# Token sums among the query products, first keys in a spare bank; layer-1 low halves and a fourth head's scaling on GpSimd

## The chip, the cores and the metric

The kernel runs on one core of a Trainium2 chip. The metric is the device time of one execution in microseconds (us). The engines that matter are TensorE (PE: matrix products, with PEld for the loads of its weights), VectorE (DVE), ScalarE (ACT), GpSimd (POOL) and the DMA queues, most of which SyncE (SP) issues. TensorE writes its results into eight PSUM banks.

## The reference, cut to what matters

Two layers of a decoder trunk on 512 tokens of width 1024, all in fp32. Only the parts that the change touches are shown.

```python
def rms_norm(x, g):
    y = x * rsqrt(mean(x * x, axis=-1, keepdims=True) + EPS)
    return y * g

# layer 0: q, k, v (8 heads of 64) and three convolution parts come from one projection
proj = rms_norm(x, g) @ w_in                       # 1024 -> 3*512 + 3*512
a_out = stick_breaking_attention(heads(q), heads(k), heads(v))
b_out = short_conv_mixer(b_gate, c_gate, u, conv_w)
x = x + concatenate([a_out, b_out]) @ w_out
x = x + swiglu(rms_norm(x, g2))                     # hidden width 2816

# layer 1: 16 query heads, 4 key/value heads of 64, an indexer that selects keys
q, k = rms_norm(q, q_gain), rms_norm(k, k_gain)     # per head of 64
score = sum_h w_idx[h] * relu(q_idx[h] @ k_idx.T)   # causal; the top 128 keys of each query count
logits = q @ k.T * HEAD_DIM ** -0.5 + rel_bias      # others -inf
p = softmax(logits)
x = x + (p @ v) @ w_out
x = x + swiglu(rms_norm(x, g3))
```

## The kernel before

**Products in halves.** Every fp32 matrix is split into a high half (rounded to fp32r) and a low half (what the rounding left), and each product is made of three TensorE products: high by high, high by low, low by high (`mm3`, L104). So for each operand there is one operation that makes the high half, a cast on ScalarE, and one that makes the low half, a subtraction, mostly on VectorE. Weights arrive by DMA in a tile `raw` (three buffers, pool `wraw`); `halves` (L159) makes `wh` on ScalarE (L163) and `wl` on VectorE (L164), three buffers each. `plan` and `split_next` split the weights of the next projection ahead of time.

**Banks.** Projections take PSUM banks in turn from a list, `self.banks` ('dbca' from here on); `few_banks(...)` sets another list. Beside a, b, c and d there are o and t, which attention uses, and two buffers z.

**Order.** In the start of layer 0 and in the mixer of layer 1 the order on TensorE, VectorE, ScalarE and GpSimd is the written one (`manual_schedule(engines=L1_ORDER)`); elsewhere a scheduler orders. Written order is made with slots: `self.after(n, fn, key)` runs fn n slots later, among others that are due by the key. Names such as LAG_TQ are such numbers.

**Start of layer 0.** `queries` (L411) transposes the tokens chunk by chunk (`turn_x`, L399), splits each chunk and accumulates four query products in the banks d, b, c and a, over five spans of chunks, whose weights `halves(i)` splits. Then `first_rstd` (L451) sums the squares of each token on VectorE (L458, four sums of a 128x1024 block), and makes the reciprocal root `rcol` and four diagonal blocks from it (L462 to L469). `stack` (L481) then moves the query products into the arena: high halves by ScalarE (L487), low halves by VectorE (L491), two of each to a bank. The first keys (`k_proj(0)`), the values V (`proj_tm(W, 1024, ...)`, evacuated by ScalarE L188 and VectorE L189) and the other keys follow. `first_rbc`, `setup_rest` and `bias_table` are small products and copies of the setup between them.

**Mixer of layer 1.** The blocks of keys/values and of two halves of the queries (`hf` 0 and 1) come out of `proj_tm` and are copied by ScalarE (`ev_kv` L996, `ev_q0`). `squares` (L933) makes the sums of squares of each head: below the limit `SQ_ACT` with one ScalarE square and accumulator for each head, above it with one square of the block and a VectorE reduction (L954, L955). `norm` scales each block by the heads' roots on GpSimd (L975). Then `turn_k` (L1012) and `turn_q` (L1028) transpose by TensorE into bank t or o (`pt`, L987) and make both halves of the result:

```python
if K_POOL:                      # turn_k; before: K_POOL is False
    src = sp.tile([P, S], F32, name="qt", tag="tmp", bufs=1)
    nc.scalar.activation(src, pt, AF.Copy, scale=gk)
    nc.scalar.copy(kh[:, g], src)
    nc.gpsimd.tensor_tensor(kl[:, g], src, khf[:, g], op=ALU.subtract)
    return
nc.scalar.activation(kh[:, g], pt, AF.Copy, scale=gk)                 # L1020
self.after(LAG_KLO, lambda: nc.vector.scalar_tensor_tensor(           # L1021
    kl[:, g], pt, gk, khf[:, g], op0=ALU.mult, op1=ALU.subtract), -1)
```

In `turn_q` a column c in `Q_POOL[hf]` goes the same way, by a ScalarE copy `qt` and a GpSimd low half (L491 in `stack`); the others read `pt` on VectorE. VectorE searches the top keys at that time (L922, L925; the masks L928).

The attention of layer 1 runs over 16 steps n, four query blocks for each of four key heads; a step has four heads r. `logits` (L1055) loads the bias of a head when its first block comes (L1066, on SP's queue, four buffers), makes z and adds bias and maximum on VectorE (L1073); `exps` is on ScalarE; `norms` (L1086) scales each head by its reciprocal sum (L1090), on GpSimd for r in `NORM_POOL` (L1093), on ScalarE for r in `NORM_ACT` (L1096), else on VectorE (L1098). `turn_p` (L1101) transposes the four heads on TensorE (L1106), and `prod` multiplies by V.

Of the kernel before, what the change touches and what calls it, by code (L numbers as in the profile page):

```python
# [8 lines left out]
F32 = mybir.dt.float32  # L9
F32R = mybir.dt.float32r  # L10
ALU = mybir.AluOpType
# [4 lines left out]
P = 128  # L16
S = 512
D = 1024
KC = D // P
TB = S // P  # L20
# [9 lines left out]
LAG_Z = 14  # L30
PRE, PRE_CUT, PRE_STORE = 20, 8, 5
LAG_K, T1P, B2, LAG_KLO, P1 = 2, 3, 'adbc', 2, 0
EARLY, SQ_ACT = 3, 0
DOT_PACE = 1
DBL_ACT, K_POOL = True, False
PACE = (4.8, 5.0, 5.3)
NORM_POOL, NORM_ACT = (1,), (3,)
Q_POOL = ((1,), (2, 3))
# [7 lines left out]
EARLY = 2  # L46
T1P = 4
LAG_K = 3
NORM_POOL = (0, 1)
NORM_ACT = (3,)  # L50
LAG_CH = 4
LAG_TQ = 5
Q_POOL = ((2,), (2, 3))
B2 = 'dbca'
LAG_N = 8
LAG_TK = 8
# [3 lines left out]
LAG_W = 4  # L60
LAG_C = 11
LAG_DOT = 5
K_POOL = False

def rel_buckets():

# [11 lines left out]
class Net:  # L78
# [329 lines left out]
        self.split(self.xh3(c), ps, g=self.g_mix(0, c))  # L408
        return lambda: nc.scalar.copy(self.xT[:, c], ps)

    def queries(self, W, raws):  # L411


        xs = self.xs
        self.qps = ps = [self.acc() for _ in range(4)]
        ws = []

        def halves(i):
            a, b = X_SPANS[i]
            raw = raws[i] if i < 3 else self.load_raw(W[a * P:b * P, 0:512].rearrange(  # L420
                "(k p) n -> p k n", p=P), b - a, 512)
            ws.append(self.halves(raw, b - a, 512))

        def dot(i, ms):
            a, b = X_SPANS[i]
            for m in ms:
                c = slice(m * P, (m + 1) * P)
                for k in range(a, b):
                    h, l = xs[k]
                    self.mm3(ps[m], ws[i][0][:, k - a, c], ws[i][1][:, k - a, c], h, l, k == 0,  # L430
                             k == KC - 1)

        keep = self.turn_x(0)
        halves(0)
        keep1 = self.turn_x(1)
        keep()
        halves(1)
        keep1()
        for i in range(5):
            dot(i, (0, 1))  # L440
            n = 2 + 2 * i
            if n < KC:
                keep = self.turn_x(n)
            dot(i, (2, 3))
            if n < KC:
                keep1 = self.turn_x(n + 1)
                keep()
                halves(i + 2)
                keep1()

    def first_rstd(self, xp):  # L451

        nc = self.nc
        xt = self.x_tm
        ss = xp.tile([P, TB], F32, name="ss")
        junk = xp.tile([P, D], F32, name="junk")
        for tb in range(TB):
            nc.vector.tensor_tensor_reduce(out=junk, in0=xt[:, tb], in1=xt[:, tb], scale=1.0,  # L458
                                           scalar=0.0, op0=ALU.mult, op1=ALU.add,
                                           accum_out=ss[:, tb:tb + 1])  # L460
        t = xp.tile([P, TB], F32, name="t4")
        nc.vector.tensor_scalar(ss, ss, 1.0 / D, EPS, op0=ALU.mult, op1=ALU.add)  # L462
        nc.scalar.activation(self.rcol, ss, AF.Abs_reciprocal_sqrt)
        self.newton(self.rcol, ss, t)
        nc.vector.tensor_scalar(self.rq[:, 0:TB], self.rcol, -0.125, None, op0=ALU.mult)
        nc.vector.tensor_scalar(self.rq[:, TB:], self.rcol, 0.125, None, op0=ALU.mult)
        dg = self.cst.tile([P, S], F32, name="sqx", tag="sqx")
        for tb in range(TB):
            nc.vector.tensor_scalar(dg[:, tb * P:(tb + 1) * P], self.ident,  # L469
                                    self.rcol[:, tb:tb + 1], None, op0=ALU.mult)  # L470
        return dg
# [128 lines left out]
    def layer0_mix(self):  # L600
# [8 lines left out]
        with self.tc.tile_pool(name="xin", bufs=1) as xp:  # L609

            raws = self.load_x(xp, W)
            with self.tc.manual_schedule(engines=L1_ORDER):
                self.queries(W, raws)
                self.plan(self.fm_tiles(W, 512, P, KC, P, 8, 1, None))
                dg = self.first_rstd(xp)
                for m in range(4):
                    qs = self.R(32 + 4 * m, 2, S)
                    self.stack([(qs[0][:, e], qs[1][:, e]) for e in range(2)], self.qps[m])
                    heads.append(qs[0])
# [8 lines left out]
        with self.tc.tile_pool(name="l0", bufs=1) as sp:  # L628
# [5 lines left out]
            def k_proj(i):  # L634
                b = 64 + 8 * (i % 3)
                (kd, kdf), kl = self.R(b, 2, S), self.R(b + 4, 2, S)[0]

                def ev_k(m, ps):
                    kt = sp.tile([P, S], F32, name="kt", tag="ct0")
                    nc.vector.tensor_tensor(kt, ps, self.rbc, op=ALU.mult)  # L640
                    for e in range(2):
                        own, oth = slice(64 * e, 64 * e + 64), slice(64 - 64 * e, 128 - 64 * e)
                        nc.scalar.copy(kd[own, e], kt[own])
                        nc.gpsimd.tensor_copy(kd[oth, e], kt[own])
                        nc.vector.tensor_tensor(kl[own, e], kt[own], kdf[own, e], op=ALU.subtract)
                self.proj_fm(W, 512 + i * P, P, xs, ev_k, gcols=P, per=8)
                return kd, kl
# [38 lines left out]

            st = self.stream(self.stick(heads, keys, sp, state), RATE0)
            for i in range(4):
                keys.append(k_proj(i))
                self.after(LAG0, more_keys)  # L690
                if i == 0:
                    self.proj_tm(W, 1024, xs, ev_v)
                    self.after(LAG0, lambda: state.update(v=True))
                    self.few_banks("ad")
                    state["acc"] = True
# [132 lines left out]
    def layer1_mix(self):  # L828
# [15 lines left out]
        with ExitStack() as es:  # L844
# [167 lines left out]
            def turn_k(g):  # L1012
                pt = turn(kn, g, "to"[g % 2])
                if K_POOL:
                    src = sp.tile([P, S], F32, name="qt", tag="tmp", bufs=1)
                    nc.scalar.activation(src, pt, AF.Copy, scale=gk)
                    nc.scalar.copy(kh[:, g], src)
                    nc.gpsimd.tensor_tensor(kl[:, g], src, khf[:, g], op=ALU.subtract)
# [4 lines that stand above are left out]
# [5 lines left out]
            def turn_q(qn, hf, c, tag):  # L1028
                pt = turn(qn, c, tag)

                if c in Q_POOL[hf]:
                    src, eng = sp.tile([P, S], F32, name="qt", tag="tmp", bufs=1), nc.gpsimd
                    nc.scalar.copy(src, pt)
                else:
                    src, eng = pt, nc.vector
                self.stack([(qs[:, h], qsf[:, h]) for h in (8 * hf + 2 * c, 8 * hf + 2 * c + 1)],
                            src, eng, LAG_LO)
# [190 lines left out]
```

## Time and profile before

| | |
|---|---|
| median of 3 runs | 1220.45 us (1219.55 to 1222.16) |
| profiled execution | 1221.7 us, its span 1219.8 us |
| TensorE busy | 1191.4 us, 98% |
| TensorE weight loads | 981.4 us, 80% |
| VectorE busy | 661.2 us, 54% |
| ScalarE busy | 477.8 us, 39% |
| GpSimd busy | 118.1 us, 10% |
| mean granted TensorE clock | 0.994 |

The times of the runs are those of whole executions. The profile is of one execution, and its span runs from the first to the last instruction. Busy time is summed over the span, so it tells how full an engine is on the whole and not which engine holds up the others at a place; that is read from the timeline and from the waits. The granted clock is given as a share of the full one; 0.50 is the lower of the two levels.

### The profile page before, as it was taken

The page shows a single profiled execution, that of the slowest core. Times are in us where ns is not written, and L with a number is a line of the kernel's source. Part 1 is how long each engine was busy: PE and PEld are TensorE (multiplying, and loading weights), DVE is VectorE, ACT ScalarE, POOL GpSimd, SP SyncE. Part 2 cuts the span into 40 slices and gives each one's busy share as a digit, 9 for nine tenths or more (in the row PEclk, how much of TensorE's full clock was granted, in tenths as well). Part 3 has the DMA queues.
Part 4 walks back from the last instruction along what each step waited for, and adds up shares of the span by engine and source line. Part 5 has one row for each costly group of instructions (what it writes and reads, how often), then busy time and mean ns, then how long its engine had stood idle before and what let it go on. Part 6 is the DMA issues. An engine that isn't in the chain of part 4 may idle for free.

```text
span 1219.8 us, 14608 instructions
## 1 busy us (share of the span) xinstructions
PE 1191.4 (98%) x5547; PEld 981.4 (80%) x5547; DVE 661.2 (54%) x1081; ACT 477.8 (39%) x778; POOL 118.1 (10%) x191
## 2 busy tenths in 40 slices
PE   9899999999999999999999889999999999999998
PEld 7677778888888888888788678888888888888886
DVE  4679975665555534333379978755434344342322
ACT  5457643554343422222252279644322232322120
POOL 1135310200000000011001134112000000000000
PEclk9899999999999999999999999999999999999999
DMA  6231225878788632233536431213333333333330
GB/s 188 76 87 52 70 70 174 269 257 288 266 264 284 227 104 78 95 98 95 172 139 229 150 104 36 70 69 121 87 104 87 97 94 89 101 97 93 125 100 35
DMA packets 118582, 159.85 MB, mean 131 GB/s; under 512 B 6292, under 2 KB 91840, under 8 KB 118512
## 3 DMA queue, kind: packets, MB, share of 16 engines
q1 hardware_dynamic: 117712, 157.73, 40.4%
q10 hardware_dynamic: 800, 1.18, 0.3%
q8 instruction: 44, 0.72, 0.3%
q14 instruction: 26, 0.21, 0.1%
HBM read 131.00 MB, written 27.89 MB: 130 GB/s over the span
## 4 chain that ended last, share of the span: by engine, by line
PE 87%; DVE 8%; issue 2%; ACT 2%; POOL 1%; POOLq 0%; DVEq 0%; ACTq 0%
PE acc L106 22%; PE acc L108 21%; PE acc L107 21%; PE acc L234 5%; PE acc L235 5%; PE acc L233 5%; DVE w L922 1%; PE z L500 1%; PE pt L1106 1%; PE z L501 1%; DVE L L925 1%; PE po L107 1%; DVE om L525 1%; PE po L108 1%; PE po L106 1%
## 5 line engine op out<-in xcount | busy, mean ns | idle before, releaser
L106 PE MATMUL acc<-arena,wh 128*128 128x512 f32 (+2 forms) x1176 | 466.5, 397 | 7.5 <-DVE arena L491 5.6
L108 PE MATMUL acc<-arena,wl 128*128 128x512 f32 (+2 forms) x1176 | 460.7, 392 | 0.1
L107 PE MATMUL acc<-arena,wh 128*128 128x512 f32 (+2 forms) x1176 | 458.9, 390 | 0.0
L164 DVE TENSOR_TENSOR wl<-raw,wh 128x1024 fp32r<-128x1024 f32 (+1 forms) x167 | 202.7, 1214 | 288.0 <-ACT wh L163 287.7
L163 ACT CAST wh<-raw 128x1024 fp32r<-128x1024 f32 (+1 forms) x167 | 173.1, 1037 | 360.4 <-PE acc L107 153.7
L106 PEld LDWEIGHTS acc<-arena,wh 128*128 128x128 f32 (+1 forms) x1176 | 221.5, 188 | 52.7 <-ACT arena L487 6.0
L108 PEld LDWEIGHTS acc<-arena,wl 128*128 128x128 f32 (+1 forms) x1176 | 221.1, 188 | 48.3 <-DVE wl L164 0.4
L107 PEld LDWEIGHTS acc<-arena,wh 128*128 128x128 f32 (+1 forms) x1176 | 221.3, 188 | 45.2 <-issue 0.7
L233 PE MATMUL acc<-wh,arena 128*128 128x512 f32 x272 | 108.9, 400 | 0.0
L234 PE MATMUL acc<-wl,arena 128*128 128x512 f32 x272 | 108.2, 398 | 0.0
L235 PE MATMUL acc<-wh,arena 128*128 128x512 f32 x272 | 108.0, 398 | 0.0
L235 PEld LDWEIGHTS acc<-wh,arena 128*128 128x128 f32 x272 | 51.6, 190 | 12.1
L803 DVE TENSOR_TENSOR pwl<-praw,pwh 128x1024 fp32r<-128x1024 f32 (+1 forms) x25 | 30.2, 1206 | 56.7 <-ACT pwh L802 56.7
L234 PEld LDWEIGHTS acc<-wl,arena 128*128 128x128 f32 x272 | 51.6, 190 | 11.5
L233 PEld LDWEIGHTS acc<-wh,arena 128*128 128x128 f32 x272 | 51.5, 189 | 11.4
L751 DVE TENSOR_TENSOR ft<-acc,rbc 128x512 f32<-128x512 f32 x44 | 30.1, 690 | 46.2 <-PE acc L108 46.1
L287 POOL TENSOR_TENSOR ssq<-ssq,sqx 128x512 f32<-128x512 f32 x12 | 18.2, 1516 | 371.7 <-ACT sqx L286 371.7
L802 ACT CAST pwh<-praw 128x1024 fp32r<-128x1024 f32 (+1 forms) x25 | 25.9, 1035 | 69.0 <-DMA praw<-in_od_w_in_dram 37.4
L753 ACT ACTIVATE fs<-ft 128x512 f32<-128x512 f32 x44 | 27.6, 629 | 51.3 <-DVE ft L751 51.2
L500 PE MATMUL z<-arena 128*128 128x384 f32 (+3 forms) x120 | 41.1, 345 | 4.6 <-DVE mx L1073 3.8
L758 DVE TENSOR_TENSOR fp<-acc,fs 128x512 f32<-128x512 f32 x44 | 30.4, 691 | 24.0 <-PE acc L108 24.0
L1073 DVE CUSTOM_DVE_ANT_0 L<-z,bias 128x128 f32<-128x128 f32 (+3 forms) x64 | 30.6, 485 | 18.2 <-PE z L1072 17.4
(210 smaller groups left out, 1263.6 us busy)
## 6 DMA issues: line engine op xcount, KB each, us to landing
raw<-in_ffn_w_gate_dram SPq DMA_DIRECT2D x44, 512.0 KB, 3.8
raw<-in_ffn_w_up_dram SPq DMA_DIRECT2D x44, 512.0 KB, 3.8
raw<-in_ffn_w_down_dram SPq DMA_DIRECT2D x42, 512.0 KB, 3.6
l1h<-pwh SPq DMA_DIRECT2D x24, 512.0 KB, 2.7
l1l<-pwl SPq DMA_DIRECT2D x24, 512.0 KB, 3.0
wh<-l1h SPq DMA_DIRECT2D x24, 512.0 KB, 4.4
wl<-l1l SPq DMA_DIRECT2D x24, 512.0 KB, 4.3
raw<-in_ev_w_in_dram SPq DMA_DIRECT2D x23, 512.0 KB, 3.8
```

The costliest lines, as they stand in the source:

```text
L106: mm(ps, wh, xh, start=first, stop=False)
L107: mm(ps, wh, xl, start=False, stop=False)
L108: mm(ps, wl, xh, start=False, stop=last)
L163: nc.scalar.copy(wh, raw)
L164: (lo or nc.vector).tensor_tensor(wl, raw, wh.bitcast(F32), op=ALU.subtract)
L233: mm(ps[tb], h[:, t], wh[:, k], start=c == 0, stop=False)
L234: mm(ps[tb], h[:, t], wl[:, k], start=False, stop=False)
L235: mm(ps[tb], l[:, t], wh[:, k], start=False, stop=c == kc - 1)
L500: self.nc.tensor.matmul(z, qs, kd, start=True, stop=False)
L758: nc.vector.tensor_tensor(p, ps, sil[m], op=ALU.mult)
L803: nc.vector.tensor_tensor(l, raw, h.bitcast(F32), op=ALU.subtract)
L1073: nc.vector.tensor_tensor_reduce(out=u["ls"][:, r], in0=z, in1=bias[h][:, 0:nk][:, ::-1], scale=1.0, scalar=FILL, op0=ALU.add, op1=ALU.max ...
```

## The change

1. The four sums of squares become a function `sums`, called in `queries` after the second and the third span, two sums each. `first_rstd` uses what they leave.
2. The first keys (i = 0) are accumulated in bank o instead of the next bank in turn, and V starts at the first bank of the list.
3. The first weight of V is split ahead together with the weight of the first keys.
4. `SQ_ACT` goes from 0 to 256: the squares of the key heads are made with ScalarE's accumulator, head by head.
5. `K_POOL` is switched on: the low halves of the keys are made by GpSimd from a ScalarE copy. All four columns of the first query half go the same way (`Q_POOL`). The copies `qt` lie in the buffers of the raw weights instead of a buffer of their own.
6. The scaling of the fourth head (r = 3) goes from ScalarE to GpSimd.

```diff
-EARLY, SQ_ACT = 3, 0
+EARLY, SQ_ACT = 3, 256
-DBL_ACT, K_POOL = True, False
+DBL_ACT, K_POOL = True, True
-NORM_POOL = (0, 1)
-NORM_ACT = (3,)
+NORM_POOL = (0, 1, 3)
+NORM_ACT = ()
-Q_POOL = ((2,), (2, 3))
+Q_POOL = ((0, 1, 2, 3), (2, 3))
-K_POOL = False
...
                 keep()
                 halves(i + 2)
                 keep1()
+            if 0 < i < 3:
+                self.sums(xp, (2 * i - 2, 2 * i - 1))
+
+    def sums(self, xp, tbs):
+
+        nc = self.nc
+        if self.ss is None:
+            self.ss = xp.tile([P, TB], F32, name="ss")
+            self.junk = xp.tile([P, D], F32, name="junk")
+        for tb in tbs:
+            nc.vector.tensor_tensor_reduce(out=self.junk, in0=self.x_tm[:, tb],
+                                           in1=self.x_tm[:, tb], scale=1.0, scalar=0.0,
+                                           op0=ALU.mult, op1=ALU.add,
+                                           accum_out=self.ss[:, tb:tb + 1])
...
-                self.plan(self.fm_tiles(W, 512, P, KC, P, 8, 1, None))
+                self.plan(self.fm_tiles(W, 512, P, KC, P, 8, 1, None)
+                          + self.tm_tiles(W, 1024, KC, None)[0:1])
...
             for i in range(4):
+                if i == 0:
+                    self.few_banks("o")
                 keys.append(k_proj(i))
+                if i == 0:
+                    self.few_banks(None)
...
-                    src = sp.tile([P, S], F32, name="qt", tag="tmp", bufs=1)
+                    src = self.wraw.tile([P, S], F32, name="qt", tag="raw")
...
-                    src, eng = sp.tile([P, S], F32, name="qt", tag="tmp", bufs=1), nc.gpsimd
+                    src, eng = self.wraw.tile([P, S], F32, name="qt", tag="raw"), nc.gpsimd
```

How the instructions stand on the engines is shown at three places. The first is VectorE at the end of the query products, before: `wl` is a weight's low half, L189 the low half of a token chunk, L458 a token sum, L462 the first step of the root.

```order
L189 SCALAR_TENSOR_TENSOR arena<-pstat,cols,arena 128x512 x2
L164 TENSOR_TENSOR wl<-raw,wh 128x1024 x2
L458 ISA junk,ss<-x_tm 128x1024
L458 ISA ss 128x1
L458 ISA junk,ss<-x_tm 128x1024
L458 ISA ss 128x1
L164 TENSOR_TENSOR wl<-raw,wh 128x1024
L458 ISA junk,ss<-x_tm 128x1024
L458 ISA ss 128x1
L458 ISA junk,ss<-x_tm 128x1024
L458 ISA ss 128x1
L462 TENSOR_SCALAR ss<-ss 128x4
```

The same place after the change, where line numbers differ a little (L460 is the sum, L163 the weight, L469 the first step of the root).

```order
L460 ISA junk,ss<-x_tm 128x1024
L460 ISA ss 128x1
L460 ISA junk,ss<-x_tm 128x1024
L460 ISA ss 128x1
L188 SCALAR_TENSOR_TENSOR arena<-pstat,cols,arena 128x512 x2
L163 TENSOR_TENSOR wl<-raw,wh 128x1024
L460 ISA junk,ss<-x_tm 128x1024
L460 ISA ss 128x1
L460 ISA junk,ss<-x_tm 128x1024
L460 ISA ss 128x1
L163 TENSOR_TENSOR wl<-raw,wh 128x1024 x2
L469 TENSOR_SCALAR ss<-ss 128x4
```

Two sums now stand ahead of the last two token chunks and two behind the last query weight; the weights of the keys and of V follow both and stand ahead of the root.

The second place is TensorE between the last query product (acc_124) and the first key product (acc_387), before, with the engines that an instruction waits for.

```order
L106 MATMUL acc_124<-arena_81,wh_256 128x512
L107 MATMUL acc_124<-arena_81,wh_256 128x512
L108 MATMUL acc_124<-arena_81,wl_257 128x512
L106 MATMUL acc_387<-arena_81,wh_311 128x512 [waits DVE_49,PE_49,Activation_49]
L107 MATMUL acc_387<-arena_81,wh_311 128x512
L108 MATMUL acc_387<-arena_81,wl_312 128x512
```

The same place after the change, where the keys' product is acc_393.

```order
L105 MATMUL acc_124<-arena_81,wh_260 128x512
L106 MATMUL acc_124<-arena_81,wh_260 128x512
L107 MATMUL acc_124<-arena_81,wl_261 128x512
L105 MATMUL acc_393<-arena_81,wh_317 128x512 [waits Activation_49]
L106 MATMUL acc_393<-arena_81,wh_317 128x512
L107 MATMUL acc_393<-arena_81,wl_318 128x512 [waits DVE_49]
```

The products stand in the same order; the first key product waits for ScalarE's half of its weight alone, and the third for VectorE's half.

The third place is GpSimd in the first six steps of the layer-1 attention, after the change: L987 scales a query block by its roots, L1105 scales a head of the attention by its reciprocal sum (L1093 before), L498 is a query's low half (L491 before).

```order
L987 TENSOR_TENSOR qn<-qn,hn_y 128x512
L1105 TENSOR_TENSOR L<-L,sm 128x128 x2
L987 TENSOR_TENSOR qn<-qn,hn_y 128x512
L1105 TENSOR_TENSOR L<-L,sm 128x128
L987 TENSOR_TENSOR qn<-qn,hn_y 128x512 x2
L1105 TENSOR_TENSOR L<-L,sm 128x256 x3
L1105 TENSOR_TENSOR L<-L,sm 128x384 x3
L1105 TENSOR_TENSOR L<-L,sm 128x512 x3
L1105 TENSOR_TENSOR L<-L,sm 128x128 x2
L498 TENSOR_TENSOR arena<-qt,arena 64x512 x2
L1105 TENSOR_TENSOR L<-L,sm 128x128
L1105 TENSOR_TENSOR L<-L,sm 128x256 x2
```

Each step has a third scaling; in the steps n = 0, 4 and 5 (for 5 behind the last row shown) it stands behind a query block's scaling or behind two low halves.

On SP's queue the first raw weights of the next part come, after the change, in between the loads of the biases; before, the twelve biases stood in one row.

```order
L1078 DMA bias<-F 128x512 x4
L155 DMA raw<-in_ffn_w_gate_dram 128x4x256
L1078 DMA bias<-F 128x512
L155 DMA raw<-in_ffn_w_gate_dram 128x4x256
L1078 DMA bias<-F 128x512 x2
L155 DMA raw<-in_ffn_w_up_dram 128x4x256
L1078 DMA bias<-F 128x512 x5
```

The three loads of raw weights that stood ahead of the mixer have moved behind the eighth, the ninth and the eleventh bias.

## Rows read from the trace of the kernel before

**Rows 1.** Window: us, PE, PEld, DVE, ACT, POOL busy (x), clock, DMA, GB/s.

```profile
0.00:1219.80 1219.80, 1191.41 (x5547) 981.37 (x5547) 661.24 (x1081) 477.77 (x778) 118.07 (x191) 0.99 0.41 131
```

**Rows 2.** Waits of TensorE: us in total, times, longest.

```profile
PE z L500 <- DVE mx L1073: 3.8, 5, 1.1
```

**Rows 3.** Timeline of TensorE, end of queries: start us, us, instruction, idle before.

```profile
34.50 0.39 PE L107 MATMUL acc<-arena,wh 128*128 128x512 f32 x1
34.73 0.40 PE L108 MATMUL acc<-arena,wl 128*128 128x512 f32 x1
40.68 0.77 PE L106 MATMUL acc<-arena,wh 128*128 128x512 f32 x1 [5.55 <-DVE arena L491]
```

**Rows 4.** Windows behind two waits of TensorE, same columns as in rows 1.

```profile
40.60:44.66 4.06, 3.98 (x10) 3.14 (x10) 3.96 (x6) 1.50 (x3) 0.00 (x0) 0.50 0.08 17
700.10:703.50 3.40, 3.33 (x10) 2.80 (x11) 3.29 (x7) 1.82 (x3) 0.77 (x1) 0.50 0.00 0
```

**Rows 5.** Timeline of VectorE, from the last query weight to the stacked queries.

```profile
24.88 0.75 DVE L189 SCALAR_TENSOR_TENSOR arena<-pstat,cols,arena 128x512 fp32r<-128x512 f32 x1 [2.45 <-ACT arena L188]
26.30 1.23 DVE L164 TENSOR_TENSOR wl<-raw,wh 128x1024 fp32r<-128x1024 f32 x1 [0.67 <-ACT wh L163]
...
28.87 1.22 DVE L458 CUSTOM_DVE_ANT_0 junk<-x_tm 128x1024 f32<-128x1024 f32 x1
...
39.14 5.65 DVE L491 TENSOR_TENSOR arena<-acc,arena 64x512 fp32r<-64x512 f32 x8
```

**Rows 6.** Timeline of ScalarE at the reciprocal root.

```profile
35.99 1.28 ACT L463 ACT_TABLE_LOAD   x1
```

**Rows 7.** Timeline of VectorE at the last block of V.

```profile
78.77 0.75 DVE L189 SCALAR_TENSOR_TENSOR arena<-acc,rcol,arena 128x512 fp32r<-128x512 f32 x1 [0.65 <-ACT arena L188]
```

**Rows 8.** Timeline of TensorE at two turns of layer 1.

```profile
674.00 0.66 PE L987 MATMUL pt<-eye,qn 128*128 128x128 f32 x4 [1.71 <-DVE arena L1021]
...
700.17 1.09 PE L987 MATMUL pt<-eye,qn 128*128 128x128 f32 x4 [2.50 <-DVE arena L491]
```

**Rows 9.** Groups of GpSimd, 690 to 780 us: busy us, mean ns, idle before.

```profile
L975 POOL TENSOR_TENSOR qn<-qn,hn_y 128x512 f32<-128x512 f32 x8 | 8.1, 1043 | 34.7 <-DVE hn_y L971 34.7
L491 POOL TENSOR_TENSOR arena<-qt,arena 64x512 fp32r<-64x512 f32 x6 | 7.9, 1321 | 9.5 <-ACT arena L487 9.1
...
L1093 POOL TENSOR_TENSOR L<-L,sm 128x256 f32<-128x256 f32 x6 | 3.6, 613 | 9.0 <-DVE sm L1090 9.0
L1093 POOL TENSOR_TENSOR L<-L,sm 128x128 f32<-128x128 f32 x6 | 2.3, 411 | 7.9 <-DVE sm L1090 7.9
```

**Rows 10.** Timeline of GpSimd in the steps 0, 4 and 5.

```profile
719.51 3.05 POOL L975 TENSOR_TENSOR qn<-qn,hn_y 128x512 f32<-128x512 f32 x3
...
739.99 2.65 POOL L491 TENSOR_TENSOR arena<-qt,arena 64x512 fp32r<-64x512 f32 x2
...
747.18 2.66 POOL L491 TENSOR_TENSOR arena<-qt,arena 64x512 fp32r<-64x512 f32 x2
```

**Rows 11.** Timeline of TensorE: transposes of the steps 0, 4, 5 and 7.

```profile
719.78 0.60 PE L1106 MATMUL pt<-eye,L 128*128 128x128 f32 x4
...
742.29 0.60 PE L1106 MATMUL pt<-eye,L 128*128 128x128 f32 x4
...
748.78 0.60 PE L1106 MATMUL pt<-eye,L 128*128 128x128 f32 x4
...
757.50 0.55 PE L1106 MATMUL pt<-eye,L 128*128 128x128 f32 x3 [0.39 <-POOL L L1093]
```

**Rows 12.** The tile `bias`: its readers, and the time its loads take.

```profile
L1073 DVE CUSTOM_DVE_ANT_0 L<-z,bias x64: 273/475/693, 711.6 to 798.6; 128x128 f32<-128x128 f32 x16, 128x256 f32<-128x256 f32 x16, 128x384 f32<-128x384 f32 x16, 128x512 f32<-128x512 f32 x16
...
DMA to landing us min/median/max: 3.1/3.2/3.6
```

**Rows 13.** VectorE's scaling of the third head: ns min/median/max, first and last start.

```profile
L1098 DVE TENSOR_SCALAR L<-L,sm x16: 279/412/1324, 719.0 to 805.0; 128x128 f32<-128x128 f32 x4, 128x256 f32<-128x256 f32 x4, 128x384 f32<-128x384 f32 x4, 128x512 f32<-128x512 f32 x4
```

**Rows 14.** Timeline of ScalarE at a block of keys.

```profile
656.74 0.37 ACT L998 COPY qn<-acc 128x256 f32<-128x256 f32 x1 [0.38 <-PE acc L235]
```

More of the change, by code (lines that the diff above doesn't have):

```diff
@@ L409, in turn_x, with queries @@
         return lambda: nc.scalar.copy(self.xT[:, c], ps)
-    def queries(self, W, raws):
+    def queries(self, W, raws, xp):
         xs = self.xs
@@ L431, in dot @@
                              k == KC - 1)
+        self.ss = None
         keep = self.turn_x(0)
@@ L449, in queries @@
                 keep1()
-    def first_rstd(self, xp):
[L453 to L460, printed above, removed]
+            if 0 < i < 3:
[10 more added lines that the diff above has]
+                                           accum_out=self.ss[:, tb:tb + 1])
+    def first_rstd(self, xp):
+        nc, ss = self.nc, self.ss
         t = xp.tile([P, TB], F32, name="t4")
@@ L612, in layer0_mix @@
             with self.tc.manual_schedule(engines=L1_ORDER):
-                self.queries(W, raws)
-                self.plan(self.fm_tiles(W, 512, P, KC, P, 8, 1, None))
+                self.queries(W, raws, xp)
+                self.plan(self.fm_tiles(W, 512, P, KC, P, 8, 1, None)
+                          + self.tm_tiles(W, 1024, KC, None)[0:1])
                 dg = self.first_rstd(xp)
```

## The prediction

> **What bounds the kernel now.** I read the whole span first: TensorE is busy 1191.41 of 1219.80 us, VectorE 661.24, ScalarE 477.77 and GpSimd 118.07 [rows 1]. So only time in which TensorE stands still, or runs at a low clock, can be won, and that is little. Next I read the waits of TensorE and went to the long ones in the timeline. Three of them lie where this change works.
>
> The longest is at the first keys of layer 0. The last query product starts at 34.73, products start 0.23 us apart, and the first key product starts only at 40.68 [rows 3]: 40.68 − 34.96 = 5.72 us are lost. TensorE waits there for a PSUM bank. The four query products fill d, b, c and a, and VectorE empties them with eight low halves from 39.14 to 44.79 [rows 5]. Behind the wait the granted clock is 0.50 for 4.06 us, that is the lower of the two levels [rows 4].
>
> The other two lie at the turns of layer 1. At 674.00 TensorE has waited 1.71 us for a key's low half on VectorE, at 700.17 2.50 us for a query's low half [rows 8]. Behind the second the clock is 0.50 for 3.40 us [rows 4].
>
> **A. Sums, spare bank, weights (layer 0).** After the last query product nothing of bank d, b, c or a is needed by the first keys, since they go to "o". What is left to hold them is their weight. On VectorE the low half of the last query weight starts at 26.30 and takes 1.23 [rows 5], until 27.5; two sums of 1.22 and a read bring it to 30.1, the key weight's low half to 31.3, the first V weight's to 32.5. TensorE wants the keys' at 34.96. It is there.
>
> The other two sums go into a stretch in which VectorE has just been idle 2.45 us until 24.88 [rows 5], and the query splits behind them are wanted only by the last 24 query products (34.96 − 24 × 0.23 = 29.4). I cost them at nothing; without that cover it would be 2.5 us.
>
> The keys take 24 × 0.23 = 5.5 us, so V starts at 40.5 and asks for d, b, c and a. The sums are complete at 32.5. Before, an activation table load of 1.28 us at 35.99 stood behind a cast [rows 6]; it now waits for nothing but ScalarE. From the end of that load, 37.27, the root and its steps on VectorE took until 39.14, 1.87 [rows 5, 6]; after the sums and 0.2 for the mean that ends at 34.6, and eight lows of 5.65 / 8 = 0.71 free a bank each 1.4 us: d 36.0, b 37.4, c 38.8, a 40.3 [rows 5]. If the table load were not hidden it would be 41.6 for a, which V's fourth token block still comes after. V therefore does not stall. Gain 5.72.
>
> As TensorE no longer stands still, the low clock behind the wait should go too: half of 4.06, 2.0 us. Between nothing and 2.0 I take 2.0, since the clock was full in the products just before.
>
> A new wait: the second keys start in bank a, where now V's last block lies. Its low half runs on VectorE from 78.77 for 0.75, behind ScalarE's half of it [rows 7]. TensorE has some small products between. The wait lies between 0 and 0.75; I take 0.3. A: −5.72 − 2.0 + 0.3 = **−7.4**.
>
> **B. Low halves on GpSimd (layer 1).** For keys and first queries ScalarE now copies the transposed block out of PSUM, and that copy frees the bank; the low half is made from the copy by GpSimd. So neither 1.71 nor 2.50 is waited for VectorE any more, which stands in the top-k search there. ScalarE is busy 39% of the span [rows 1], and one copy and one cast per turn take the place of one cast. GpSimd takes 1.32 for a 64x512 low [rows 9], against 0.71 on VectorE [rows 5]. Eight of them are 10.6 us; four key lows, of the same columns, lie between four times 1.04 and four times 1.32 [rows 9]. The query lows start near 697 and the heads that are wanted first, 0 to 3, are done some 5.3 us later; the first logits are read near 711.6 [rows 12]. Covered; without that cover each would be worth up to 0.6, 4.9 in all. The 3.40 us at clock 0.50 [rows 4] lose half, 1.70, when the idle time ahead of them goes. B: −1.71 − 2.50 − 1.70 = **−5.9**.
>
> **Squares of the key heads.** Sixteen small ScalarE squares take the place of four of a 128x256 block, and four VectorE reductions go. A 128x256 copy is 0.37 and ScalarE sits idle 0.38 before it [rows 14]. Four squares of 64 columns lie between 0.37 and 4 × 0.37 = 1.48 a block, at most 1.1 more than before, 0.7 beyond the idle time. After the fourth block ScalarE would be 2.9 us late; its next bank is wanted only when 18 products (4.1 us) have passed. Nothing.
>
> **C. The fourth head's scaling on GpSimd (layer 1 attention).** Of the four scalings of a step n (a key head and a query block) GpSimd takes heads 0, 1 and now 3; ScalarE loses sixteen. GpSimd takes 0.41 for 128x128, 0.61 for 128x256 and, by the equal-sized product of L975, 1.04 for 128x512 [rows 9]. It is mostly idle, so in most steps the third is done in time. It is late where other GpSimd work stands ahead of it. The transposes of a step take 0.60 for four, so the fourth starts 0.33 after the first [rows 11]:
> - n=0: one L975 from 719.51 [rows 10] stands between: 719.51 + 1.04 + 0.41 = 720.96, wanted 719.78 + 0.33 = 720.11. 0.85 late.
> - n=4: two lows 739.99 + 2.65 [rows 10], + 0.41 = 743.05, wanted 742.62. 0.43.
> - n=5: 747.18 + 2.66 + 0.61 = 750.45, wanted 749.11. 1.34.
> - n=7: the second scaling already holds TensorE 0.39 at 757.50 [rows 11]; the third comes 1.04 behind it, wanted 0.22 behind. 0.8.
>
> Together 3.4. A late step delays the later ones less than in full, because VectorE's maximum now makes TensorE wait 3.8 us in five places [rows 2], of which some passes meanwhile; I take 0.7 off. The bounds are 0 and about 8 (below). C: **+2.7**.
>
> VectorE's own scaling, the third head's, can get slower beside a busier GpSimd: it takes 412 ns in the middle and once 1324 [rows 13]. By the rows I cost this at nothing, since those tails exist already and TensorE waits on none of them. The Trainium skill, "SBUF — State Buffer", section "SBUF: two separate sides", says that VectorE (in some modes, or with two SBUF inputs) and GpSimd share a pair of ports as an exclusive lock, so that the loser stands still for a whole instruction. The 1324 agrees with this, and by that rule each of 16 steps could lose up to one GpSimd scaling (0.4 to 1.0), 10 us in all, so the sum would be about nothing instead of −10.6; this is a rival below.
>
> **Sum.** −7.4 − 5.9 + 2.7 = −10.6. The profiled execution took 1221.7, span 1219.8; 1211.1 by its own time. The median of the runs shown, 1220.45, is 1.25 below that execution, which gives **1209.8**.
>
> **Rivals.**
> - *Attention gives nothing back* (C = 0): −13.3, 1207.1. For it: ScalarE has 16 scalings fewer, and exponents come earlier. Against it: four places above where the third scaling is late by its own row.
> - *GpSimd becomes the releaser in all of the attention*: 16 steps by 0.5 (a 128x256 scaling less what slack there is) = 8 instead of 2.7: 1215.1. For it: n=7 waits for GpSimd before the change. Against: it is idle for several us in most steps.
> - *The gap at the first keys only moves*: V then stands for bank a or c, because the scale comes as late as before. The lows would end 44.8 instead of 40.3; about 5 of 7.4 are lost: 1214.8.
> - *Ports*: each of the sixteen steps loses 0.6 in VectorE's scaling behind GpSimd's, and the top-k search beside eight more lows the rest: some 10 us, 1219.8, no change. By [rows 13] the middle of 412 says that most steps do not meet.
> - *Slower*: the copies lie in the buffers of raw weights, so three feed-forward loads of 512 KB move on SP's queue to between the bias loads, each waiting until GpSimd has freed its buffer. A bias takes 3.2 us to land [rows 12]. If the biases behind each of the three loads come late by one landing (9.6) and each idle stretch costs the clock as the one at 700.17 did (3 × 1.7 = 5.1), it is −10.6 + 14.7 = +4.1: 1224.5. It decides from 3.5 us a load (10.6 over three). Against: only the last of them waits for a low (749.84) [rows 10], and a landing of 3.2 us behind it could make one bias late by some tenths.
>
> **How the numbers follow.** Forecast 0.55 (own range 1207.8 to 1212.5); nothing given back 0.13; GpSimd throughout 0.14; gap moves 0.08; ports 0.05; slower 0.05. From no change 0.2% (2.4 us, about what a measurement of this kernel can tell) is 1218.0 to 1222.9: faster 0.90, same 0.05, slower 0.05. The range for 8 in 10 reaches over the forecast and most of the two cases beside it: 1205.8 to 1215.5.
>
> **What the profile after would show.** A: no wait over 1 us between the queries and the keys, clock full there, the eight lows from about 34.6; wrong if V waits for L491's line. B: no wait of TensorE at the turns on VectorE; wrong if it waits there for ScalarE's copies or GpSimd's lows. C: waits of the transposes on GpSimd at n=0, 4, 5 and 7, 2 to 4 us in all; wrong if they are spread over all steps, or if TensorE waits for a bias in z. The prediction falls most easily by C, or by a clock that drops at another place.

## The result

| | before | changed |
|---|---|---|
| median of 5 runs | 1220.53 us | 1212.62 us |
| lowest to highest | 1219.55 to 1222.16 | 1211.93 to 1215.94 |
| profiled execution / its span | 1221.7 / 1219.8 | 1214.13 / 1212.4 |

The ratio is 0.994, 95% interval 0.9924 to 0.9956: 7.9 us faster by the medians (5 to 9 by the interval). The forecast was 1209.8 with a range from 1205.8 to 1215.5. One later execution of the kernel before took 2395.55 us and is left out of all medians.

The page of the changed kernel, the line of its span and the busy times:

```profile
span 1212.4 us, 14654 instructions
PE 1189.0 (98%) x5547; PEld 978.5 (81%) x5547; DVE 652.9 (54%) x1067; ACT 480.1 (40%) x797; POOL 143.8 (12%) x217
```

GpSimd has taken over 26 us and VectorE lost 8, but what counts are TensorE's waits. The view of its waits, with us in total, times and the longest:

```profile
PE z L507 <- DVE mx L1085: 4.1, 6, 1.1
PE pt L1118 <- POOL L L1105: 3.3, 5, 1.3
...
PE z L507 <- POOL arena L652: 1.8, 1, 1.8
```

The wait for a bank at the first keys is gone [rows 3], and both waits at the turns [rows 8]. Two have come: five on GpSimd's scalings, 3.3 us (one of 0.4 before, [rows 11]), and one of 1.8 in layer 0 that no step of the prediction named, on GpSimd's copy of the first keys.

**A's gain, and what is given back of it.** The first key product starts right behind the last query product; in TensorE's timeline:

```profile
33.59 0.39 PE L107 MATMUL acc<-arena,wl 128*128 128x512 f32 x1
33.82 0.39 PE L105 MATMUL acc<-arena,wh 128*128 128x512 f32 x1
```

Windows of the changed kernel, columns as in rows 1:

```profile
33.00:41.00 8.00, 8.00 (x37) 6.53 (x36) 7.43 (x12) 4.02 (x7) 0.00 (x0) 1.00 0.22 77
52.40:55.40 3.00, 3.00 (x10) 2.37 (x9) 1.69 (x4) 1.52 (x5) 1.19 (x6) 0.53 0.56 163
742.20:745.00 2.80, 2.80 (x14) 2.80 (x15) 2.34 (x9) 2.60 (x8) 1.61 (x2) 0.50 0.47 167
```

From 33 to 41 us TensorE is busy without a gap at full clock; the low clock of [rows 4] is gone there. But two new stretches at the lower level have come, behind the two new waits: about half of 3.0 and of 2.8 us are lost in them. In layer 1 there was a second one before as well: beside the stretch of [rows 4], one behind TensorE's waits for the first maxima, where the changed kernel runs at full clock. A window of before:

```profile
713.60:717.20 3.60, 3.30 (x13) 2.83 (x14) 2.70 (x18) 2.95 (x9) 0.35 (x1) 0.53 0.52 211
```

What holds TensorE at 51.62, in the timelines of four engines (ACTq is ScalarE's DMA queue):

```profile
45.32 0.32 ACTq L383 DMA_DIRECT2D F<-ft  x1
49.28 0.69 DVE L648 TENSOR_TENSOR kt<-acc,rbc 128x512 f32<-128x512 f32 x1 [2.90 <-DMA F<-ft]
49.89 1.22 DVE L163 TENSOR_TENSOR wl<-raw,wh 128x1024 fp32r<-128x1024 f32 x1
50.11 2.49 POOL L652 CAST arena<-kt 64x512 fp32r<-64x512 f32 x2 [0.33 <-DVE kt L648]
51.62 0.50 PE L507 MATMUL z<-arena 128*128 128x128 f32 x2 [1.76 <-POOL arena L652]
```

Read it backwards: the first scores wait for GpSimd's copy of the keys; that for the keys' scaling `kt` on VectorE; that for a transfer F<-ft, issued 45.32, that writes the bias table to memory (with the table in a place of its own this wait is gone, see below). The same two places in the kernel before:

```profile
54.49 0.69 DVE L640 TENSOR_TENSOR kt<-acc,rbc 128x512 f32<-128x512 f32 x1 [1.62 <-DMA F<-ft]
56.18 0.39 PE L500 MATMUL z<-arena 128*128 128x128 f32 x2
```

TensorE is ready for the first scores at 51.62 − 1.76 = 49.86 instead of 56.18, 6.3 us sooner, although the scheduler now puts ten more of V's products ahead of them. `kt` comes only 5.2 us sooner, and the copy behind it takes longer than before (last section). About 1.1 of both is the start of the execution, as follows.

**Not all of the profiles' difference is the change's.** The same small products at the program's start run at different speed in the two executions; a window of before, then of the changed kernel:

```profile
1.00:8.00 7.00, 6.88 (x34) 6.74 (x35) 0.75 (x4) 1.58 (x2) 3.14 (x7) 1.00 0.82 257
```

```profile
1.00:8.00 7.00, 6.53 (x39) 6.14 (x39) 0.79 (x5) 2.33 (x4) 3.15 (x7) 1.00 0.77 246
```

Five more products fit into the same 7 us. By TensorE's thirty-first instruction the changed kernel is 1.14 us ahead, though neither engine nor order differs there. It starts at 7.5 and 6.4 us here and between 6.2 and 7.6 in the twelve kernels below, whose start is the same, so this is chance of one execution, and a difference of two profiles is known only to about a microsecond. The medians average over it.

### The profile page after: what moved, and what is told of

It reads as the page before. It is cut to its first block, busy times and chain, and to the rows that moved or that the text cites. A ratio compares the mean times of both kernels' runs of the same rounds, so it can differ in the third digit from the quotient of the medians.

```text
span 1212.4 us, 14654 instructions
## 1 busy us (share of the span) xinstructions
PE 1189.0 (98%) x5547; PEld 978.5 (81%) x5547; DVE 652.9 (54%) x1067; ACT 480.1 (40%) x797; POOL 143.8 (12%) x217
## 4 chain that ended last, share of the span: by engine, by line
PE 89%; DVE 6%; issue 2%; POOL 2%; ACT 0%; DMA 0%; POOLq 0%; DVEq 0%; ACTq 0%
PE acc L105 22%; PE acc L107 21%; PE acc L106 21%; PE acc L234 6%; PE acc L233 6%; PE acc L232 6%; PE pt L1118 1%; PE z L507 1%; PE z L508 1%; DVE om L532 1%; DVE wl L163 1%; PE po L106 1%; PE po L107 1%; DVE be L535 1%; PE po L105 1%
## 5 line engine op out<-in xcount | busy, mean ns | idle before, releaser
L163 DVE TENSOR_TENSOR wl<-raw,wh 128x1024 fp32r<-128x1024 f32 (+1 forms) x167 | 202.9, 1215 | 285.3 <-ACT wh L162 285.0
```

What stands on the lines that cost most here:

```text
L163: (lo or nc.vector).tensor_tensor(wl, raw, wh.bitcast(F32), op=ALU.subtract)
```

## The experiments

Differences are of medians, each against the kernel before in its own comparison (1221.28, 1221.44, 1221.31 and 1220.94 us).

**Layer 0 alone.** The change without its layer-1 parts:

```diff
-EARLY, SQ_ACT = 3, 256
-DBL_ACT, K_POOL = True, True
-NORM_POOL = (0, 1, 3)
-NORM_ACT = ()
-Q_POOL = ((0, 1, 2, 3), (2, 3))
+EARLY, SQ_ACT = 3, 0
+DBL_ACT, K_POOL = True, False
+NORM_POOL = (0, 1)
+NORM_ACT = (3,)
+Q_POOL = ((2,), (2, 3))
```

> Only the part in layer 0 (sums among the query products, first keys in bank o, first V weight ahead); layer 1 as before. Theory: this part wins 7.7 us at the first keys and gives 3.0 back at the first attention scores, where the product waits for GpSimd's copy of the first keys (1.9 us) and then runs at a low clock (1.1): about -4.5 us against before, and the wait on GpSimd is there although layer 1 is unchanged. Rival: the wait comes from something else in the changed kernel, then this part alone gives the -7.4 us of the prediction.

1214.54 us, −6.7, ratio 0.9938 (0.9926 to 0.9951). The wait on GpSimd is there with layer 1 unchanged, 1.3 us, so it belongs to this part; my −4.5 was too small, because it counted a stretch of low clock behind the wait that this execution does not have:

```profile
PE z L507 <- POOL arena L652: 1.3, 1, 1.3
```

**Turns alone.** Keys' and queries' low halves on GpSimd with the copies in the raw buffers; everything else as before (the opposite of the diff above, with NORM_POOL, NORM_ACT and SQ_ACT as before).

> Only the low halves of keys and first queries on GpSimd, with their copies in the raw-weight buffers; layer 0, the squares and the fourth head's scaling as before. Theory: the two waits at the turns (1.7 and 2.5 us) and the low clock behind the second go: -6 us against before, and no wait of the attention on the bias loads. Rival: three large loads between the biases cost something in the attention, then less than -5.

1216.20 us, −5.1, ratio 0.9953 (0.994 to 0.9965). Both waits at the turns are gone. The rival has a part: VectorE waits for biases. The tile `bias`, this kernel:

```profile
  DMA bias<-F: 2.3, 2
...
DMA to landing us min/median/max: 3.1/4.4/6.0
```

Before, no engine waited for a bias, and landing took 3.2 in the middle and 3.6 at most [rows 12]. The longest says little: with layer 0 alone, where the queue is as before, it is 6.0 as well, with 3.2 in the middle and no wait.

**Fourth head's scaling back on ScalarE**, in the changed kernel:

```diff
-NORM_POOL = (0, 1, 3)
-NORM_ACT = ()
+NORM_POOL = (0, 1)
+NORM_ACT = (3,)
```

> The changed kernel with the fourth head's scaling back on ScalarE. Theory: the scaling on GpSimd costs 3 to 4 us (late at steps 0, 4, 5 and 7, with a low clock behind step 5), so this kernel is 3 to 4 us faster than the changed one, -11.5 against before. Rival: ScalarE's scalings hold the next exponents, so it gives nothing: -8 against before.

1210.11 us, −11.2, ratio 0.9903 (0.9889 to 0.9916). The changed kernel stands at −7.9, so the scaling on GpSimd costs 3.3 us (2.5 by the two kernels' own medians, 1212.62 and 1210.11; the intervals of the ratios do not meet). Of TensorE's waits on GpSimd's scalings one is left, the one that was there before [rows 11]:

```profile
PE pt L1118 <- POOL L L1105: 0.3, 1, 0.3
```

**The bias table in a place of its own**, in the changed kernel:

```diff
+        self.ftp = self.tc.tile_pool(name="ftp", bufs=1)
+        fp = self.ftp.__enter__()
...
-            ft = bp.tile([16, 640], F32, name="ft")
+            ft = fp.tile([16, 640], F32, name="ft")
```

> The changed kernel with the bias table's rows (ft) in a place of their own, so that the first keys' scaling on VectorE needn't wait until their transfer to memory has landed (49.2 us). The scheduler then puts the first attention scores eight products (1.9 us) earlier. Theory: the wait for that transfer is what makes the first keys late; they come 2.3 us earlier, and 1 to 3 us are won against the changed kernel. Rival: as the scores are put earlier too, the wait for GpSimd's copy stays as long and nothing is won.

1213.11 us, −8.2, against −7.9: no difference. The keys do come earlier, `kt` at 47.38 and the first scores at 48.91 without a wait. But TensorE now waits for the low half of the attention's weights, at 62.00 in the same attention:

```profile
PE pt L554 <- DVE be L537: 2.1, 5, 0.6
PE pt L554 <- DVE wtl L185: 1.2, 1, 1.2
```

The second row is new. The transfer does hold the keys, as the theory said; that the time hangs on it falls. The wait moved along.

**Both**, scaling back and table in its own place:

> The changed kernel with the fourth head's scaling on ScalarE and the bias table's rows in a place of their own. Theory: the two do not touch each other, so what the second gave alone (0.3 us, nothing that can be told) is what it gives here: -11.4 us against before. Rival: the scores that the scheduler puts earlier start the attention of layer 0 earlier for good, then -13.

1210.16 us, ratio 0.9912 (0.9898 to 0.9926), −11.3: as without the second edit.

**Squares as before**, with the scaling on ScalarE (`SQ_ACT = 0`):

> As the kernel with the fourth head's scaling on ScalarE, and the key heads' squares as before (one square of a block on ScalarE, one reduction on VectorE). Theory: the squares lie beside TensorE's products and cost nothing either way: -11.2 us against before, within 1 us. Rival: VectorE's four reductions stand in the top-k search and delay it, or ScalarE's sixteen squares hold a bank: 1 to 2 us of difference.

1209.76 us, −11.7, ratio 0.9912 (0.9898 to 0.9926): no difference that can be told from the 1210.11 with the new squares. Nothing, as the prediction had it.

**Second half's copies in a buffer of their own**, with the scaling on ScalarE:

```diff
-                    src, eng = self.wraw.tile([P, S], F32, name="qt", tag="raw"), nc.gpsimd
+                    src, eng = (self.wraw.tile([P, S], F32, name="qt", tag="raw") if hf == 0 else
+                                sp.tile([P, S], F32, name="qt", tag="tmp", bufs=1)), nc.gpsimd
```

> As the kernel with the fourth head's scaling on ScalarE, but the copies of the second query half lie in a buffer of their own as before, so that the three loads of raw weights come ahead of the biases on SP's queue again. Theory: the loads between the biases make biases late (landing 4.4 us in the middle and 6.0 at most, against 3.2 and 3.6 before; VectorE stood 2.3 us for them) and cost about 1 us: -12.2 us against before, no wait of VectorE for a bias. Rival: those waits are hidden, and the time lost in the attention is the clock's: -11.2, no difference.

1208.62 us, −12.8, ratio 0.9898 (0.9883 to 0.9914), the fastest median of the study. No engine waits for a bias any more. Against the kernel with the scaling back that is 1.6 us by the medians, and 1.1 against the kernel with the squares as before, timed beside it; expected 1.0. The intervals overlap, and the last kernel below, where no engine waits for a bias either, is only 0.5 faster than the one with the scaling back. So that the late biases cost about 1 us is likely and not shown.

**All copies in one buffer of their own.** By a slip this kernel kept the scaling on GpSimd (it is the changed kernel with `tag="tmp", bufs=1` for every `qt`), so it is to be read against the changed kernel's −7.9 and not as its expectation says.

> As the kernel with the fourth head's scaling on ScalarE, with all copies qt in one buffer of their own instead of three raw-weight buffers; the raw loads stay ahead of the biases. Theory: the turns are some 3 us apart and GpSimd needs 2.7 for both lows of one, so one buffer nearly does; it costs nothing to 1 us at the turns and saves the 1 us of late biases: -11.5 to -12.9 against before. Rival: ScalarE's copy waits for GpSimd and holds TensorE at each turn: -9.

1218.78 us, −2.5, ratio 0.9982 (0.9973 to 0.9991): 5.4 us slower than with the raw buffers. ScalarE's next copy waits until GpSimd has made both low halves of the last, in ScalarE's timeline, and the first scores pay for it, in TensorE's waits:

```profile
699.24 0.59 ACT L1045 COPY qt<-pt 128x512 f32<-128x512 f32 x1 [2.11 <-POOL arena L498]
```

```profile
PE z L507 <- DVE mx L1085: 7.8, 4, 5.8
```

Behind that copy ScalarE's squares of the second half stand, behind these VectorE's reductions, and behind these the first maxima, 5.8 us late. So GpSimd's 1.32 for a low half [rows 9] is covered with three buffers for the copies and not with one; two were not tried.

**Scaling on ScalarE in four steps only**:

```diff
-                    if r in NORM_POOL:
+                    if r in NORM_POOL and not (r == 3 and n in (0, 4, 5, 7)):
...
-                    elif r in NORM_ACT:
+                    elif r == 3:
```

> The changed kernel, but in the steps n = 0, 4, 5 and 7 the fourth head is scaled on ScalarE; in the other twelve on GpSimd. Theory: the cost of the scaling on GpSimd is made in these four steps alone, so all of it (3.3 us) comes back: -11.2 us against before, at least as fast as with all sixteen on ScalarE. Rival: the twelve others cost too, by ports or by waits that move: -9 to -10.

1210.76 us, −10.7, ratio 0.9915 (0.9903 to 0.9928). Of the 3.3 us 2.8 come back by moving four of sixteen scalings. The other twelve cost nothing that can be told. Of TensorE's waits on GpSimd's scalings little is left:

```profile
PE pt L1118 <- POOL L L1105: 0.5, 2, 0.3
```

**The spare bank alone**, and then **the sums alone** (with the first V weight ahead), in the kernel before:

```diff
+                if i == 0:
+                    self.few_banks("o")
                 keys.append(k_proj(i))
+                if i == 0:
+                    self.few_banks(None)
```

> The kernel before with nothing changed but the bank of the first keys (o); the sums and the first V weight stay where they were. Theory: it is the bank that wins. The key weight is ready at 32.5 us, and the four lows, though they still run from 39.1 to 44.8, free a bank just when V comes to it (1.4 us apart, from 40.5 on), so V loses a few tenths: -6 us against before, like the whole part in layer 0 (-6.7). Rival: the sums had to go first, V stalls until 44.8, about 4 us: -2.

1215.67 us, −5.6, ratio 0.9954 (0.9942 to 0.9967). The eight lows run as late as the theory had them, and V waits for no bank; a window of this kernel, and VectorE's timeline:

```profile
34.00:45.00 11.00, 10.93 (x47) 8.32 (x46) 9.45 (x22) 8.11 (x12) 0.00 (x0) 1.00 0.26 79
```

```profile
38.19 5.66 DVE L491 TENSOR_TENSOR arena<-acc,arena 64x512 fp32r<-64x512 f32 x8
```

> The kernel before with the sums among the query products and the first V weight ahead, but the first keys in the next bank in turn as before. Theory: the lows start near 34 and free bank d 1.4 us later, so the keys wait 1 us instead of 5.6; the low clock behind the wait may go or stay: -4 to -6 us against before. Rival: without the spare bank the wait stays long, because ScalarE's and VectorE's halves of the first bank come only after the root: -2 or less.

1213.32 us, −8.0, ratio 0.9936 (0.9924 to 0.9949). Each edit alone wins most or all of the part; both together (−6.7) are not better than the sums alone. With the sums alone the keys wait a little, and the first scores not at all; TensorE's and GpSimd's timelines:

```profile
35.14 0.47 PE L105 MATMUL acc<-arena,wh 128*128 128x512 f32 x1 [0.60 <-DVE arena L498]
...
50.96 0.47 PE L507 MATMUL z<-arena 128*128 128x128 f32 x2
```

```profile
50.25 1.76 POOL L652 CAST arena<-kt 64x512 fp32r<-64x512 f32 x2 [0.33 <-DVE kt L648]
```

**The best parts together**: no spare bank, scaling on ScalarE, second half's copies in their own buffer.

> The changed kernel without its spare bank, with the fourth head's scaling on ScalarE, and with the second query half's copies in a buffer of their own. Theory: the spare bank adds nothing once the sums have gone ahead (sums alone -8.0, sums and bank -6.7, intervals overlapping), so this is as fast as the same kernel with the bank (1208.6, -12.9) or up to 1.3 us faster; the wait of 1.4 us on GpSimd's copy of the first keys goes and one of 0.6 at the first keys comes. Rival: the bank is worth its 0.6 us: -12.

1209.27 us, −11.7, ratio 0.9904 (0.9887 to 0.992), against 0.9898 with the bank: the same. The spare bank is worth nothing that can be told once the sums have moved, and costs nothing either.

## Why the prediction was right, and 2.7 us too large

The direction and the mechanism of all three terms hold; by the medians each term was taken too well, and the errors add up. Measured by kernels that do one part, or undo it:

| term | predicted | measured | by |
|---|---|---|---|
| A, layer 0 | −7.4 | −6.7 | that part alone |
| B, turns | −5.9 | −5.1 | that part alone |
| C, fourth head | +2.7 | +3.3 | undone: −11.2 against −7.9 |
| sum | −10.6 | −7.9 | the change |

The measured three make −8.5, within what medians can tell of −7.9. By their intervals A lies between −9.0 and −6.0 and B between −7.3 and −4.3, and C is 2.5 to 3.3 by the two ways to take it, so no term by itself is shown to be off; the whole is (5.4 to 9.3 us won, 10.6 forecast). Where the rest went is read from the waits.

**A.** The gain of 5.72 + 2.0 is there: keys start at once, the clock stays full, V does not stall, the lows run from 33.05. The step that was mis-sized is "A new wait": 0.3 for the second keys in bank a. That wait does not come. In its place the first scores wait, 1.2 to 1.8 us in the kernels with sums, bank and the table in its old place. I followed each operation to the end of V and did not ask what else comes sooner: the products of the first scores, whose keys hang on the transfer of the bias table. Their scaling on VectorE was waiting for it before as well (1.62 us, shown above), unseen, since TensorE came later.

That A would need both edits I took for granted, in saying that nothing of bank d, b, c or a is needed by the keys. The runs show that moving the sums does most of it alone, since the lows then start before the keys want a bank and the keys wait 0.60 us; and that the bank does most of it alone.

**B.** Both waits went as worked out, and the cover for GpSimd's low halves held, but not with one buffer. The term that was not safe is the clock's 1.70: it was the price in one execution. With layer 0 alone the second turn still waits 2.49 us, and the clock behind it is full; TensorE's timeline and a window of that kernel:

```profile
693.75 0.63 PE L999 MATMUL pt<-eye,qn 128*128 128x128 f32 x4 [2.49 <-DVE arena L498]
```

```profile
692.00:696.00 4.00, 2.25 (x12) 1.71 (x13) 3.87 (x8) 1.47 (x3) 0.15 (x1) 1.00 0.00 0
```

It is full there with the sums alone too, and low with the bank alone, so with the kernel before the profiles show two executions of each kind. Half of 1.70 would make B −5.06, near the −5.1 measured; that this is the reason is not shown. The attention may give something back besides: with the turns alone VectorE waits 2.3 us for two biases behind loads of 512 KB, in the changed kernel itself 0.5 us for one. That was the rival "slower", whose price I put at one landing for each of three loads; if it came true, then at a tenth of that, about 1 to 2 us.

**C.** The four places were right: TensorE waits at steps 0, 4, 5 and 7. In the changed kernel at step 5, GpSimd's and TensorE's timelines:

```profile
735.39 1.19 POOL L1105 TENSOR_TENSOR L<-L,sm 128x256 f32<-128x256 f32 x2 [3.38 <-DVE sm L1102]
736.66 2.65 POOL L498 TENSOR_TENSOR arena<-qt,arena 64x512 fp32r<-64x512 f32 x2
739.38 0.61 POOL L1105 TENSOR_TENSOR L<-L,sm 128x256 f32<-128x256 f32 x1
```

```profile
740.05 0.33 PE L1118 MATMUL pt<-eye,L 128*128 128x128 f32 x1 [1.29 <-POOL L L1105]
```

The scaling stands behind two low halves and comes 1.29 us late, worked out as 1.34. At the four steps the third scaling holds TensorE 0.70, 0.39, 1.29 and 0.56 us, 2.9 in all; the sum had 3.4 for them less 0.7, so by the waits it was nearly met. What it had not counted is the clock, which falls for 2.8 us behind the longest wait in this execution. That can't be put down to the scaling: with the table moved the same wait is there (1.27 us at 740.08), the clock behind it is full, and a low stretch lies earlier. Two windows of that kernel:

```profile
703.20:706.40 3.20, 3.14 (x11) 2.88 (x12) 2.04 (x14) 2.61 (x9) 1.04 (x1) 0.50 0.25 102
740.00:745.00 5.00, 4.30 (x31) 3.77 (x32) 3.57 (x13) 4.39 (x11) 2.54 (x4) 1.00 0.69 216
```

With the scaling back on ScalarE there is such a stretch too, from 703.2 to 706.6 at 0.52. Why the clock falls behind one wait of 1.3 us and not behind another stays open.

**The rivals.** That the attention gives nothing back falls with the 2.5 to 3.3 us of C. GpSimd as the releaser throughout the attention falls: moving four scalings brought 2.8 of 3.3 us back. A gap that only moves came true in part, at the scores and for other reasons than V's banks: with the bank alone the scale came late and V stood for no bank, so the price of that rival was wrong. The ports did not decide the time: VectorE's scaling of the third head took 9.8 us in its sixteen steps before and 9.8 after, though they show in one place, below. The line of that scaling in the changed kernel, to compare with [rows 13]:

```profile
L1110 DVE TENSOR_SCALAR L<-L,sm x16: 282/427/1324, 707.2 to 797.7; 128x128 f32<-128x128 f32 x4, 128x256 f32<-128x256 f32 x4, 128x384 f32<-128x384 f32 x4, 128x512 f32<-128x512 f32 x4
```

## What to carry to other kernels

When a wait is taken away, follow what arrives earlier because of it, not only what is edited: the next product downstream can hang on a chain (here a small table's transfer) that was always that late and never seen. Work moved to an idle, slower engine costs nothing where it has slack and everything where other work of that engine stands just ahead of it; list these places one by one from its timeline, since moving four of sixteen back was enough. A low clock behind a wait in one profile is not a fixed price: look whether it is there in the profiles of other kernels with the same wait. And a buffer that is borrowed from another part of the program moves that part's loads on the queue: look at the order of the DMA queue before and after.

## What the runs showed of the hardware

GpSimd's copy of the first keys is two casts of 64x512. One of them takes 0.61 us where no VectorE subtraction of two SBUF inputs is under way when it starts, and 1.47 or 1.50 where VectorE is in the low half of a weight (two inputs from SBUF, 128x1024). The changed kernel, GpSimd's timeline (VectorE's low half is the L163 shown in the section on the result):

```profile
50.11 1.47 POOL L652 CAST arena<-kt 64x512 fp32r<-64x512 f32 x1 [0.33 <-DVE kt L648]
```

The kernel with the bank alone, timelines of GpSimd and VectorE:

```profile
54.36 0.61 POOL L644 CAST arena<-kt 64x512 fp32r<-64x512 f32 x1 [0.39 <-DVE kt L640]
55.02 1.50 POOL L644 CAST arena<-kt 64x512 fp32r<-64x512 f32 x1
```

```profile
54.58 1.46 DVE L164 TENSOR_TENSOR wl<-raw,wh 128x1024 fp32r<-128x1024 f32 x1 [0.35 <-ACT wh L163]
```

The slow cast ends 0.47 us behind the end of VectorE's instruction in the one and 0.48 in the other. It loses 0.86 and 0.89 us, where 1.00 and 1.02 of VectorE's instruction were left when it started. VectorE's low half, which in the second kernel starts while the first cast runs, takes 1.46 instead of 1.22. The two casts together take 1.76 in the kernel before, with the turns alone, with the sums alone, with the table moved (both kernels) and in the last kernel, where a weight's low half does not follow at once (about 0.61 for the first and 1.10 for the second, beside VectorE's low half of the keys, 64x512); and 2.48 or 2.49 in the changed kernel, with layer 0 alone, and in the five others with sums, bank and the table in its old place.

The Trainium skill, "SBUF — State Buffer", section "SBUF: two separate sides", has the two engines lock a shared pair of ports for a whole instruction, where VectorE has two SBUF inputs and GpSimd reads SBUF, so that the one that comes second stands still. The trace agrees in that the cast loses nearly all that is left of VectorE's instruction, while VectorE lost 0.24 us where 0.39 of the cast was left. Without the 0.86 the copy in the changed kernel would have ended at 50.72 and not at 51.58, so by an estimate from these rows that is about half of the 1.76 us that the first scores wait; no run took it apart from the order of VectorE's work.
